# Key latent and narrow columns in one product, and the query latent's norm applied in the softmax's exponential

## Chip, cores and metric

The kernel runs on one core of one Trainium2 chip. The metric is the device time of one execution in microseconds; of several executions the median counts. PE is the matmul engine, PEld its weight load, DVE the vector engine, ACT the scalar (activation) engine, POOL the general engine, SP the engine that issues most DMAs.

## What is computed

Two layers of a trunk with three branches (a state space mixer, latent attention, a gated delta rule), all fed by one input projection of the normed input, 512 tokens by 1024 channels, float32. The change is in latent attention (MLA) and in the projection's columns that feed it:

```python
xn = rmsnorm(x, norm1_g)
proj = xn @ w_in                        # columns: ... c_q 512, c_kv 256, k_rope 64, dt 16, a 8, b 8 ...
q  = (rmsnorm(cq, q_norm_g)   @ w_uq)   # 8 heads of 128 + 64 (rotary)
kv = (rmsnorm(ckv, kv_norm_g) @ w_ukv)  # 8 heads of 128 (key) + 128 (value)
sc = (q_nope @ k_nope.T + rope(q_pe) @ rope(k_rope).T) * (128 + 64) ** -0.5
o  = softmax(causal(sc)) @ v
```

## The kernel before, in words

Every matrix product is made in three parts (L181 to L183, helper `mm3`): a value is split into a high part (ACT, L153 for weights) and a low part (DVE, L154), and high x high, high x low and low x high are summed. Weights come by DMA into `wraw` (two buffers) and are split into `whi` and `wlo` (four buffers each, 512 columns). The normed input stands transposed, features on partitions, as eight tiles `xh`, `xl`, one for each 128 features.

`dense_T` (L217) yields a product with tokens on partitions: the input's 128 tokens are the stationary side, the weights' columns move past. `dense_F` (L187) yields it with features on partitions: 128 weight columns are stationary, all 512 tokens move.

A layer starts with the norm of the input in two halves of 256 tokens (`norm_half`, L286): scaling on DVE (L291), transposes on PE (L296), the split into `xh` (ACT, L260) and `xl` (DVE, L261). To have work while the second half is normed, PE makes with the first half the product of 96 narrow columns (`smalls`, tile `yt`: k_rope, dt, a, b, features on partitions, 256 tokens at a time) and the first four pieces of the query latent's product (512 columns, tokens on partitions). Behind the second half's norm come the rest of the query latent, the four transposes of the narrow columns (L392), and the key latent's product (256 columns, tokens on partitions). Then `latent` (L478) norms both: squares summed on ACT (L485), the scale on DVE and POOL (L264, L265), the scaling on DVE (L489), transposes on PE (L494: 16 for the query, 8 for the key), and a split with the gain (L260, L261).

In layer 0 a table of angles is made in the same time (`rope_tables`, L119, DVE L127 to L144, two sine calls of ACT, L142 and L145), and the step sizes of the other branches are worked out (L404 to L446), from `sv`.

Latent attention follows, four pairs of heads. For each head and each of four token tiles PE makes the scores (L611 to L615) and adds the mask (L616), DVE takes the negated maximum `mx` (L620), ACT the exponential with its sum (L623), DVE the scaling (L624, L625), PE the transposes (L633), and then the product with the values (L649 to L651).

Each engine runs its own list of instructions in order. The lists are made when the kernel is built, by the framework's scheduler: it walks the program and places what it takes to be ready, weight splits with priority. So a stage of the program text can be spread between others, and what stands in a list behind a waiting instruction waits too.

Of the kernel before, what the change touches and what calls it, by code (L numbers as in the profile page):

```python
# [20 lines left out]
P = 128  # L21
# [6 lines left out]
O_SZ, O_XBC, O_DT, O_CQ, O_CKV, O_KR = 0, 1024, 2560, 2576, 3088, 3344  # L28
O_GQ, O_GK, O_GV, O_GZ, O_GB, O_GA, O_GATE = 3408, 3920, 4432, 5456, 6480, 6488, 6496
NBLK = 5  # L30
HALVES = (slice(0, S // 2), slice(S // 2, S))
# [23 lines left out]
def hybrid_kernel(ctx, tc, a, out, depth=2, taps=None):  # L55
# [33 lines left out]
    def y_bank():  # L89
        return mk(ps_sm, [P, 512], F32, "yt", 1)  # L90
# [6 lines left out]

    ct = mk(cst, [P, NBLK * P + 112], F32, "ct")
    sync.dma_start(ct[:, :P], cm[:, :P])
# [116 lines left out]

    def dense_T(gen, n, K, xh, xl, evac, cols=lambda w: w, mid=None, hook=None):  # L217

# [15 lines left out]
        if hook:  # L234
# [6 lines left out]
            return  # L241
        if mid:
            lead = [next(gen) for _ in range(4)]
            for w in lead:
                part(w, (0, 1))
            mid()
            for w in lead:
                part(w, (2, 3))
        for w in gen:
# [61 lines left out]

    def small_raw(ly):

        raw = mk(wp, [P, KD * 96], F32, "wraw", 2)
        sync.dma_start(raw, a["w_small"][ly])
        return raw

    def small_weights(raw, first=True):
        res = []
        for q in range(2):  # L320
            hold = [mk(lp, [P, 384], F32R, "mix", 8) for _ in range(2)]
            hi, lo = split_half(raw[:, q * 384 : (q + 1) * 384], hold, first)
            res.append((4 * q, hi.rearrange("p (k n) -> p k n", k=4), lo.rearrange("p (k n) -> p k n", k=4)))
        return res
# [11 lines left out]
    for t in range(T):  # L336
# [3 lines left out]
        for i in range(2):  # L340
            if t == 2 and i == 1:

                raws0 = small_raw(0), weights_raw(a["w_in"][0], O_CQ, 512, 0, 2)
# [10 lines left out]
    for ly in range(depth):  # L354
# [6 lines left out]


        sw = small_weights(small_raw(ly)) if ly else small_weights(raws0[0], False)
        ps_small = y_bank()

        def smalls(hf):
            for k0, wh, wl in sw:
                for k in range(4):
                    kk = k0 + k
                    mm3(ps_small[:96, hf], wh[:, k, :], wl[:, k, :], xh[kk][:, hf], xl[kk][:, hf], kk == 0, kk == KD - 1)  # L370

        def second_half():
            norm_half(1, [xt[:, t] for t in range(T)], ssq, lambda k: col(g_n1 + k), xpl, xh, xl)
            if ly == 0:
                load_constants()
                load_rows(prow, 0)
            smalls(HALVES[1])

        smalls(HALVES[0])
        cq_tok = [mk(lp, [P, 512], F32, "mix", 8) for t in range(T)]  # L380
        dense_T(weights(w_in, O_CQ, 512, D, raw0=None if ly else raws0[1]), 512, D, xh, xl, lambda t, ps: act.copy(cq_tok[t], ps), mid=second_half)
# [6 lines left out]
        smT = mk(ml, [96, S], F32, "qp")  # L388
        act.copy(smT, ps_small[:96, :])
        ps = sm_bank()  # L390
        for t in range(T):
            pe.transpose(ps[:, t * P : t * P + 96], smT[:, t * P : (t + 1) * P], ident[:96, :96])  # L392
        sv = mk(ml, [P, T, 32], F32, "sv")
        dve.tensor_copy(sv, ps.rearrange("p (t n) -> p t n", t=T)[:, :, 64:96])

# [101 lines left out]

        ck_tok = [mk(lp, [P, 256], F32, "mix", 8) for t in range(T)]
# [14 lines left out]

        kd = mk(lp, [P, S], F32, "mix", 8)
        for i in range(2):
            act.dma_start(kd[64 * i : 64 * i + 64], smT[:64])
        kpe = rope(kd)
# [16 lines left out]
        for hp in range(4):  # L534
# [67 lines left out]
            for j in range(2):  # L602
# [3 lines left out]
                for t in range(T):  # L606
# [655 lines left out]
def lay_out(inputs):  # L1262
# [6 lines left out]
    res["prows"] = np.concatenate([v[n] for n in ROWS], axis=1)  # L1269
    w = np.concatenate([v["w_in"][:, :, c : c + n] for c, n in ((O_KR, 64), (O_DT, 16), (O_GA, 8), (O_GB, 8))], axis=2)  # L1270
    res["w_small"] = np.ascontiguousarray(w.reshape(depth, KD, P, 96).transpose(0, 2, 1, 3)).reshape(depth, P, KD * 96)
    res["cmats"] = shape_constants()
# [17 lines left out]
```

## Time and profile before

| | us |
|---|---|
| median of 3 executions | 2338.18 (2336.49 to 2344.52) |
| span of the profiled execution | 2334.6 |
| PE busy in it | 2294.8 |
| DVE busy | 1582.1 |
| ACT busy | 1159.8 |
| PE waits for latent norms, layer 0 and layer 1 | 2.5 and 1.3 |

The profiled execution is a further one, known by its span from first to last instruction alone; the three timed executions include what lies around the span. The granted matmul clock was 0.996 of full speed in it. How to read: a timeline row has the start, the duration, engine, line, operation, output and inputs, shapes and count, and in brackets the idle time of the engine ahead of it with what ended that. A matmul's duration overlaps the next one's, so a busy PE is not PE at its peak. A waits row has the sum, the count and the longest. SPq is the queue of DMA issues on SP.

### The profile page before, as it was taken

Reading aid. Unit: us, or ns where it says so; the run is one execution under the profiler, and the core shown is the slowest. Engines: PE = TensorE matmul, PEld = TensorE weight load, DVE = VectorE, ACT = ScalarE, POOL = GpSimd, SP = SyncE. Lnnn points to the kernel's source line nnn. Section 1 sums busy time; section 2 is a strip of 40 time slices with the busy share of each in tenths; the row PEclk is TensorE's granted clock in tenths of the full one; section 3 lists DMA queues with packets and bytes.
Section 4 is the critical chain, followed back from the end, with each engine's and each line's share of the span. In section 5 each row is a group of like instructions: output and inputs, shape, how many; then the busy total and the mean of one; then the engine's idle time right before and its main releaser. Section 6 shows DMA issues by size and latency. Waiting matters only on the chain.

```text
span 2334.6 us, 32156 instructions
## 1 busy us (share of the span) xinstructions
PE 2294.8 (98%) x11926; PEld 1891.3 (81%) x11926; DVE 1582.1 (68%) x3100; ACT 1159.8 (50%) x2403; POOL 58.6 (3%) x74
## 2 busy tenths in 40 slices
PE   8999999999999999999999999999999999999998
PEld 7788787878887888888888887888788878888886
DVE  6776656875675458668767765667756645677668
ACT  6656644333443345545656557443334434545545
POOL 0000000000000000000010000000000000000000
PEclk9999999999999999999999999999999999999999
DMA  4323533352222443243132235334422224333231
GB/s 136 87 63 92 169 101 109 109 154 73 86 69 72 140 150 108 73 127 108 44 101 81 82 91 170 101 105 139 118 82 86 68 77 158 126 118 100 91 109 46
DMA packets 208221, 240.38 MB, mean 103 GB/s; under 512 B 33920, under 2 KB 155456, under 8 KB 208064
## 3 DMA queue, kind: packets, MB, share of 16 engines
q1 hardware_dynamic: 204544, 233.07, 32.7%
q10 hardware_dynamic: 3520, 5.25, 0.9%
q8 instruction: 94, 1.54, 0.3%
q14 instruction: 63, 0.52, 0.1%
HBM read 221.41 MB, written 11.63 MB: 100 GB/s over the span
## 4 chain that ended last, share of the span: by engine, by line
PE 86%; DVE 7%; DMA 3%; ACT 2%; POOL 1%; issue 1%; ACTq 0%; SPq 0%; DVEq 0%; POOLq 0%
PE acc L181 22%; PE acc L182 22%; PE acc L183 22%; PE sm L183 2%; PE sm L182 2%; PE sm L181 2%; DVE wlo L154 1%; PE sm L730 1%; DMA eE<-d_c 1%; DVE tok L846 1%; DMA mix<-mix 1%; PE sm L633 1%; DVE gQ L845 1%; PE yt L182 1%; PE sm L1003 1%
## 5 line engine op out<-in xcount | busy, mean ns | idle before, releaser
L154 DVE TENSOR_TENSOR wlo<-wraw,whi 128x512 fp32r<-128x512 f32 x552 | 378.3, 689 | 429.2 <-ACT whi L153 412.4
L153 ACT CAST whi<-wraw 128x512 fp32r<-128x512 f32 x552 | 341.4, 621 | 598.0 <-PE acc L182 371.0
L183 PE MATMUL acc<-xh,wlo 128*128 128x512 f32 (+1 forms) x1184 | 460.9, 390 | 0.0
L181 PE MATMUL acc<-xh,whi 128*128 128x512 f32 (+1 forms) x1184 | 460.7, 390 | 0.0
L182 PE MATMUL acc<-xl,whi 128*128 128x512 f32 (+1 forms) x1184 | 460.0, 389 | 0.0
L183 PEld LDWEIGHTS acc<-xh,wlo 128*128 128x128 f32 x1184 | 223.6, 189 | 41.9
L182 PEld LDWEIGHTS acc<-xl,whi 128*128 128x128 f32 x1184 | 223.5, 189 | 42.0 <-DVE xl L261 0.4
L181 PEld LDWEIGHTS acc<-xh,whi 128*128 128x128 f32 x1184 | 223.2, 189 | 41.7 <-ACT xh L260 0.4
L181 PE MATMUL acc<-yh,whi 128*128 128x512 f32 x384 | 151.9, 399 | 0.0
L182 PE MATMUL acc<-yl,whi 128*128 128x512 f32 x384 | 151.4, 394 | 0.0
L183 PE MATMUL acc<-yh,wlo 128*128 128x512 f32 x384 | 151.3, 394 | 0.0
L183 PE MATMUL acc<-whi,xl 128*128 128x512 f32 (+1 forms) x384 | 144.0, 375 | 0.0
L182 PE MATMUL acc<-wlo,xh 128*128 128x512 f32 (+1 forms) x384 | 143.9, 375 | 0.0
L181 PE MATMUL acc<-whi,xh 128*128 128x512 f32 (+1 forms) x384 | 142.6, 374 | 0.0
L674 DVE SCALAR_TENSOR_TENSOR ckl<-acc,pc,ckl 128x511 f32<-128x511 f32 (+2 forms) x168 | 120.4, 744 | 16.9 <-ACT ckl L670 8.3
L153 ACT CAST whi<-wr 128x512 fp32r<-128x512 f32 x128 | 79.5, 621 | 68.2 <-PE acc L183 32.7
L183 PE MATMUL acc<-whi,yl 128*128 128x512 f32 x256 | 99.7, 389 | 0.0
L181 PE MATMUL acc<-whi,yh 128*128 128x512 f32 x256 | 99.7, 389 | 0.0
L182 PE MATMUL acc<-wlo,yh 128*128 128x512 f32 x256 | 99.6, 389 | 0.0
L154 DVE TENSOR_TENSOR wlo<-wr,whi 128x512 fp32r<-128x512 f32 x128 | 85.8, 686 | 12.5 <-ACT whi L153 11.7
L181 PEld LDWEIGHTS acc<-yh,whi 128*128 128x128 f32 x384 | 71.7, 188 | 16.8 <-ACT yh L260 1.7
L182 PEld LDWEIGHTS acc<-yl,whi 128*128 128x128 f32 x384 | 72.2, 188 | 15.3 <-issue 1.0
(411 smaller groups left out, 4545.3 us busy)
## 6 DMA issues: line engine op xcount, KB each, us to landing
wraw<-in_w_in_dram SPq DMA_DIRECT2D x148, 512.0 KB, 3.6
wraw<-in_w_up_dram SPq DMA_DIRECT2D x64, 512.0 KB, 3.6
wr<-in_w_down_dram SPq DMA_DIRECT2D x32, 1024.0 KB, 5.0
eE<-d_c SPq DMA_DIRECT2D x48, 256.0 KB, 4.0
wraw<-in_w_mla_out_dram SPq DMA_DIRECT2D x16, 512.0 KB, 3.4
eE<-d_e SPq DMA_DIRECT2D x32, 256.0 KB, 3.0
wraw<-in_w_ssd_out_dram SPq DMA_DIRECT2D x16, 512.0 KB, 3.4
wraw<-in_w_gdn_out_dram SPq DMA_DIRECT2D x16, 512.0 KB, 3.3
```

Of the source, the lines that this page charges most:

```text
L153: act.copy(hi, raw)
L154: dve.tensor_tensor(lo, raw, f32(hi), ALU.subtract)
L181: pe.matmul(o, ah, bh, start=start, stop=False, skip_group_check=more)
L182: pe.matmul(o, ah, bl, start=False, stop=False, skip_group_check=more)
L183: pe.matmul(o, al, bh, start=False, stop=stop, skip_group_check=more)
L633: pe.transpose(ps[:, n : n + P], pn[t][:, kb * P : (kb + 1) * P], ident)
L674: dve.scalar_tensor_tensor(acc[:, d:], ps[:, : S - d], taps_[3 - d], acc[:, d:], ALU.mult, ALU.add)
L730: pe.matmul(py[:, h * 64 : (h + 1) * 64], e2[h // 4][:, h % 4, :], xd[:, h * 64 : (h + 1) * 64], start=True, stop=True)
L845: dve.tensor_tensor(pd, bc_last(nb[:, m, m + 1 :], m + 1), bc_mid(xb[:, m, : m + 1], 31 - m), ALU.mult)
L846: dve.tensor_tensor(xb[:, m + 1 :, : m + 1], xb[:, m + 1 :, : m + 1], pd, ALU.add)
L1003: pe.matmul(po[:, h * P : (h + 1) * P], pt_[:, h, :], vn[:, h * P : (h + 1) * P], start=True, stop=True)
```

## The change

- The 64 + 32 narrow columns are joined to the key latent's 256: one product of 352 columns, tokens on partitions, in the place of `smalls` and of the first query pieces. For tokens 0 to 255 it runs while the second half is normed, for the others after it. All eight pieces of its weights stay split: four in `mix` tiles, four in `whi` and `wlo`. The weights are laid out anew in memory (`w_front`) and come in four loads of 360 KB a layer.
- The rotary key's 64 columns are copied twice next to each other out of the product (DVE), and four transposes give the doubled tile `kd`, which two DMAs copied together before. `sv` is copied straight out of the product.
- The query latent is a `dense_F` product in two halves of 256 columns: features on partitions, no transposes. It is split with its gain but without its norm. ACT squares it, DVE adds the four squares up, PE sums them over the partitions against a column of ones, and the result is the scale of each token, `q_rs`. A query's scale is common to a row of scores, so it is applied to the maximum (a new ACT operation) and as the exponential's scale.
- The second half of the query latent's product stands behind the key latent's norm in the text.

```diff
-        sw = small_weights(small_raw(ly)) if ly else small_weights(raws0[0], False)
-        smalls(HALVES[0])
-        cq_tok = [mk(lp, [P, 512], F32, "mix", 8) for t in range(T)]
-        dense_T(weights(w_in, O_CQ, 512, D, ...), 512, D, xh, xl, lambda t, ps: act.copy(cq_tok[t], ps), mid=second_half)
...
+    def front_weights(ly, raws):
+        res = []
+        for q in range(KD // 2):
+            given = q < len(raws)
+            raw = raws[q] if given else front_raw(ly, q)
+            for i in range(2):
+                hold = [mk(lp, [P, NF], F32R, "mix", 8) for _ in range(2)] if q < 2 else None
+                res.append(split_half(raw[:, i * NF : (i + 1) * NF], hold, not given))
...
+        def front(ts):
+            pss = [acc_bank()[:, :NF] for _ in ts]
+            for k, (wh, wl) in enumerate(fw):
+                for t, ps in zip(ts, pss):
+                    tok = slice(t * P, (t + 1) * P)
+                    mm3(ps, xh[k][:, tok], xl[k][:, tok], wh, wl, k == 0, k == KD - 1)
+            for t, ps in zip(ts, pss):
+                act.copy(ck_tok[t], ps[:, :256])
+                dve.tensor_copy(kr_tok[:, t].rearrange("p (i n) -> p i n", i=2), bc_mid(ps[:, 256:320], 2))
+                dve.tensor_copy(sv[:, t], ps[:, 320:])
+        front((0, 1))
+        norm_half(1, ...)
+        front((2, 3))
...
-        dense_T(weights(w_in, O_CKV, 256, D), 256, D, xh, xl, lambda t, ps: act.copy(ck_tok[t], ps))
-        cqh, cql = latent(ml, cq_tok, 512, g_q, "cq")
+        def query_latent(i):
+            for j, ps in enumerate(dense_F(weights(w_in, O_CQ + 256 * i, 256, D), tiles(256), D, xh, xl)):
+                k = 2 * i + j
+                split_gain(cqh[k], cql[k], ps, col(g_q + k))
+                cq_sq.append(mk(ml, [P, S], F32, "pn3", 2))
+                act.activation(cq_sq[-1], ps, AF.Square)
+                if k:
+                    dve.tensor_tensor(cq_sq[0], cq_sq[0], cq_sq[k], ALU.add)
+        query_latent(0)
         ckh, ckl = latent(lp, ck_tok, 256, g_kv, "ck")
...
+        query_latent(1)
+        for t in range(T):
+            pe.matmul(ps[:, t : t + 1], cq_sq[0][:, t * P : (t + 1) * P], ones[:, 0:1], start=True, stop=True)
+        rsq(q_rs, ps[:, :T], 1.0 / 512, EPS)
...
-                    act.activation(pt_[:, :n], o, AF.Exp, bias=mx, accum_out=sm)
+                    act.activation(mx, mx, AF.Copy, scale=q_rs[:, t : t + 1])
+                    act.activation(pt_[:, :n], o, AF.Exp, bias=mx, scale=q_rs[:, t : t + 1], accum_out=sm)
```

Three places show how the lists change. The first is ACT at the start of layer 0, before: `wraw_128` holds the narrow columns, `wraw_130` and `wraw_255` the first query pieces, `hj` are squares of the input's halves.

```order
L153 CAST mix_206<-wraw_128 128x384
L153 CAST mix_210<-wraw_128 128x384
L260 ACTIVATE xh_26_142<-sm_170,pc_121 128x256
L260 ACTIVATE xh_28_144<-sm_179,pc_121 128x256
L260 ACTIVATE xh_30_146<-sm_188,pc_121 128x256
```

And in the change, where `wraw_128`, `130`, `222` and `232` are the four loads of the front, in this order:

```order
L154 CAST whi_224<-wraw_222 128x352
L154 CAST whi_228<-wraw_222 128x352
L254 ACTIVATE xh_30_146<-sm_188,pc_121 128x256
L254 ACTIVATE xh_32_148<-sm_197,pc_121 128x256
L154 CAST mix_218<-wraw_130 128x352
L415 ACTIVATE aexp_1084<-prow_123 128x24
L254 ACTIVATE xh_31_147<-sm_188,pc_121 128x256
L254 ACTIVATE xh_33_149<-sm_197,pc_121 128x256
L154 CAST whi_234<-wraw_232 128x352
L154 CAST whi_238<-wraw_232 128x352
```

The last piece of the second load (`mix_218`) stands behind both pieces of the third, and the fourth load goes into the second one's buffer, which is free when that piece is split.

The second place is PE where the latents are normed in layer 0, before: `mix_239` to `242` are the query latent's token tiles, `acc_744` to `746` the first pair of heads' queries.

```order
L494 MATMUL sm_671<-ct_75,mix_242 128x128
L181 MATMUL acc_744<-cqh_123_649,whi_749 128x512
L181 MATMUL acc_745<-cqh_123_649,whi_749 128x512
L181 MATMUL acc_746<-cqh_123_649,whi_749 128x512
L494 MATMUL sm_678<-ct_75,mix_239 128x128
```

And in the change: `acc_576` is the last tile of the query latent, `yh_68` to `yh_71` the scaled key latent, `yl_72` the rotary key.

```order
L182 MATMUL acc_576<-xh_32_148,whi_629 128x512
L487 MATMUL sm_554<-ct_75,yh_68_242 128x128
L487 MATMUL sm_561<-ct_75,yh_68_242 128x128
L507 MATMUL sm_568<-ct_75,yl_72_246 128x128
L487 MATMUL sm_554<-ct_75,yh_69_243 128x128
...
L507 MATMUL sm_568<-ct_75,yl_72_246 128x128 x3
L183 MATMUL acc_576<-xl_40_156,whi_629 128x512
```

The keys' transposes stand five products ahead of the end of the query latent's 96, and the query's transposes are gone.

The third place is ACT in the first head's softmax, before (`pn` the probabilities of a token tile, `sme` their sum):

```order
L623 ACTIVATE pn_200_930,sme_931<-sm_921,mx_928 128x128
L623 ACTIVATE pn_204_944,sme_945<-sm_935,mx_942 128x256
L623 ACTIVATE pn_208_958,sme_959<-sm_949,mx_956 128x384
L623 ACTIVATE pn_212_972,sme_973<-sm_963,mx_970 128x512
L562 ACTIVATE qh_1227<-acc_1160 128x512
```

And in the change (`qrs` is the query's scale):

```order
L634 ACTIVATE mx_869<-mx_869,qrs_660 128x1
L634 ACTIVATE mx_884<-mx_884,qrs_660 128x1
L635 ACTIVATE pn_196_871,sme_872<-sm_862,mx_869,qrs_660 128x128
L635 ACTIVATE pn_200_886,sme_887<-sm_877,mx_884,qrs_660 128x256
L557 CAST whi_1491<-wraw_1489 128x256
L634 ACTIVATE mx_899<-mx_899,qrs_660 128x1
L558 CAST whi_1491<-wraw_1489 128x128
L635 ACTIVATE pn_204_901,sme_902<-sm_892,mx_899,qrs_660 128x384
```

Each exponential has a second small instruction ahead of it on the same engine and reads what that one wrote.

More of the change, by code (lines that the diff above doesn't have):

```diff
@@ L241, in dense_T @@
             return
[L242 to L248, printed above, removed]
         for w in gen:
@@ L310, in load_rows, with front_raw @@
         sync.dma_start(prow, a["prows"][ly].partition_broadcast(P))
-    def small_raw(ly):
-        raw = mk(wp, [P, KD * 96], F32, "wraw", 2)
-        sync.dma_start(raw, a["w_small"][ly])
+    def front_raw(ly, q):
+        raw = mk(wp, [P, 2 * NF], F32, "wraw", 2)
+        sync.dma_start(raw, a["w_front"][ly][:, 2 * q * NF : 2 * (q + 1) * NF])
         return raw
-    def small_weights(raw, first=True):
+    def front_weights(ly, raws):
         res = []
[L320 to L323, printed above, removed]
+        for q in range(KD // 2):
[4 more added lines that the diff above has]
+                res.append(split_half(raw[:, i * NF : (i + 1) * NF], hold, not given))
         return res
@@ L341, in hybrid_kernel @@
             if t == 2 and i == 1:
-                raws0 = small_raw(0), weights_raw(a["w_in"][0], O_CQ, 512, 0, 2)
+                raws0 = [front_raw(0, q) for q in range(2)]
             hf = slice(i * 512, (i + 1) * 512)
@@ L387, in hybrid_kernel @@
             rope_tables(ml)
[L388 to L394, printed above, removed]
         cum = mk(sp, [P, T, 24], F32, "cum")
@@ L496, in latent @@
             return hs, ls
-        ck_tok = [mk(lp, [P, 256], F32, "mix", 8) for t in range(T)]
-        dense_T(weights(w_in, O_CKV, 256, D), 256, D, xh, xl, lambda t, ps: act.copy(ck_tok[t], ps))
-        cqh, cql = latent(ml, cq_tok, 512, g_q, "cq")
-        ckh, ckl = latent(lp, ck_tok, 256, g_kv, "ck")
+        cqh, cql = hilo_tags(ml, "cq", 4)
+        cq_sq = []
+        def query_latent(i):
[7 more added lines that the diff above has]
+        query_latent(0)
+        ckh, ckl = latent(lp, ck_tok, 256, g_kv, "ck")
+        ps = sm_bank()
+        for t in range(T):
+            pe.transpose(ps[:, t * P : (t + 1) * P], kr_tok[:, t], ident)
+        kd = mk(lp, [P, S], F32, "mix", 8)
+        act.copy(kd, ps)
+        query_latent(1)
+        ps = sm_bank()
+        for t in range(T):
+            pe.matmul(ps[:, t : t + 1], cq_sq[0][:, t * P : (t + 1) * P], ones[:, 0:1], start=True, stop=True)
+        q_rs = mk(sp, [P, T], F32, "qrs")
+        rsq(q_rs, ps[:, :T], 1.0 / 512, EPS)
         def rope(src):
@@ L512, in rope @@
             return ta
-        kd = mk(lp, [P, S], F32, "mix", 8)
-        for i in range(2):
-            act.dma_start(kd[64 * i : 64 * i + 64], smT[:64])
         kpe = rope(kd)
```

31 lines of the change are left out of this document (14 added, 17 removed).

## Prediction

> **What bounds the kernel now.** I read the engines' totals first, then the chain that ended last, then PE's waits around the two places that the change edits.
>
> ```profile
> span 2334.6 us, 32156 instructions
> PE 2294.8 (98%) x11926; PEld 1891.3 (81%) x11926; DVE 1582.1 (68%) x3100; ACT 1159.8 (50%) x2403; POOL 58.6 (3%) x74
> PE 86%; DVE 7%; DMA 3%; ACT 2%; POOL 1%; issue 1%; ACTq 0%; SPq 0%; DVEq 0%; POOLq 0%
> ```
>
> PE carries 86% of the chain and is idle for 39.8 us of 2334.6. So the change is worth what it takes from PE's own work, plus the idle stretches it closes, less those it opens. DVE and ACT matter only where PE stands still for them. PE's waits in the first stage of layer 0 (0 to 215 us), and then of layer 1 (1150 to 1370 us):
>
> ```profile
> PE sm L296 <- DVE xr L291: 1.6, 2, 1.4
> PE sm L494 <- DVE cql L261: 1.2, 1, 1.2
> PE sm L494 <- DVE mix L489: 1.0, 1, 1.0
> PE acc L181 <- ACT cqh L260: 0.3, 1, 0.3
> ...
> PE sm L494 <- DVE mix L489: 1.0, 1, 1.0
> PE acc L181 <- ACT cqh L260: 0.3, 1, 0.3
> ```
>
> The L494 and cqh rows are the latent norms: 2.5 us idle in layer 0 and 1.3 in layer 1, **3.8 us** together. Nothing here is large; the whole stake is some 0.4% of the span.
>
> **PE's work.** Durations of matmuls overlap, so a product's price is its distance to the next one. First and last row of an unbroken stretch of the old query product (66 products), and of the old key product (95):
>
> ```profile
> 29.24 0.39 PE L181 MATMUL acc<-whi,xh 128*128 128x512 f32 x1
> 43.97 0.39 PE L183 MATMUL acc<-whi,xl 128*128 128x512 f32 x1
> 44.68 0.28 PE L182 MATMUL acc<-wlo,xh 128*128 128x256 f32 x1
> 55.96 0.28 PE L183 MATMUL acc<-whi,xl 128*128 128x256 f32 x1
> ```
>
> 65 distances of 512 columns take 14.73 us, 0.227 each; 94 of 256 take 11.28, 0.120 each. A column is thus (0.227 - 0.120)/256 = 0.00042 us, and a product of 352 columns, which the trace does not show, 0.160 by interpolation. Per layer 48 narrow and 96 key products of 256 columns (17.3 us) become 96 of 352 (15.4 us): -1.9. The query product keeps its 96 products of 512 columns; only which side is stationary changes. Next, the transposes:
>
> ```profile
> 56.08 1.47 PE L494 MATMUL sm<-ct,mix 128*128 128x128 f32 x12
> 57.84 0.96 PE L181 MATMUL acc<-cqh,whi 128*128 128x512 f32 x3 [0.29 <-ACT cqh L260]
> 60.02 0.66 PE L494 MATMUL sm<-ct,mix 128*128 128x128 f32 x4 [1.22 <-DVE cql L261]
> 60.43 0.48 PE L182 MATMUL acc<-cql,whi 128*128 128x512 f32 x1
> 60.74 0.40 PE L183 MATMUL acc<-cqh,wlo 128*128 128x512 f32 x1
> 63.95 0.63 PE L494 MATMUL sm<-ct,mix 128*128 128x128 f32 x4 [0.95 <-DVE mix L489]
> L935 PE MATMUL sm<-ct,ft 128*128 128x1 f32 x64 | 7.5, 242 | 0.0
> ```
>
> Four transposes hold PE for 0.41 us (60.02 to 60.43), and the product behind them takes 0.31 in place of 0.227. Sixteen of the query latent go: -1.6 a layer. The four transposes of the narrow columns stay as four of another shape: 0. Four sums of squares against a column of ones come, shown in kind at L935 at most 0.24 each: 0 to 1.0 a layer, and I take 0.5 with the switch. In the softmax the scheduler now cuts the transposes into 35 and 34 groups for 29 and 29, 11 more switches at 0.09: +1.0. Sum: 2 x (-1.9 - 1.6 + 0.5) + 1.0 = **-5.0 us**.
>
> The Trainium skill ("TensorE: Matmul & The Clock Gate", Part 4: PE-mode transpose) gives about 275 ns for a transpose in one kernel's context. By that estimate the 32 transposes would be worth 8.8 us and not 3.2, and the result 5.6 us lower. The trace gives the same duration, but twelve end within 1.47 us, so they overlap and the distance decides.
>
> **The start of layer 0** gets worse. The front now needs all eight pieces of weights before the second half's transposes, four loads where two are in flight, and the fourth load waits for the second one's last split.
>
> ```profile
> 10.22 0.93 ACT L153 CAST mix<-wraw 128x384 fp32r<-128x384 f32 x2 [0.21 <-DMA wraw<-in_w_small_dram]
> 10.77 1.03 DVE L154 TENSOR_TENSOR mix<-wraw,mix 128x384 fp32r<-128x384 f32 x2 [0.17 <-ACT mix L153]
> 11.82 0.38 SPq L160 DMA_DIRECT2D wraw<-in_w_in_dram  x1
> DMA to landing us min/median/max: 3.1/3.8/7.0
> 23.02 1.36 PE L296 MATMUL sm<-ct,xr 128*128 128x128 f32 x11
> ```
>
> The third load leaves as at 11.8 and lands 3.1 to 3.8 later, near 15.2. In ACT's order its two casts (0.45 each) and two activations stand ahead of the cast of the fourth piece, which ends at 17.5, its subtraction on DVE at 18.1. The fourth load leaves then, lands near 21.6, and with cast and subtraction its low half is there at 22.6. Eleven products at 0.160 follow: PE reaches the transposes at 24.4 where it was at 23.02, with 7.7 us of products done where it had 8.3. New idle time: 1.4 + 0.6 = **+2.0** (0 if the load lands in the minimum and the casts wait less; 3 with a late landing). Layer 1 has its weights early; there the fourth group of transposes waits instead:
>
> ```profile
> 1174.54 0.28 PE L181 MATMUL yt<-xh,mix 128*96 128x256 f32 x1
> 1176.56 1.25 DVE L261 SCALAR_TENSOR_TENSOR xl<-sm,pc,xh 128x256 fp32r<-128x256 f32 x3
> ```
>
> From 1174.54 the new order has ten products (1.6 us) ahead of it, and the low half it waits for ends near 1177.0: **+0.9** (0 to 1.5).
>
> **The key latent's norm** is now covered by the second half of the query product, but in layer 0 its scaling stands on DVE behind the table of angles.
>
> ```profile
> 33.18 0.69 DVE L154 TENSOR_TENSOR wlo<-wraw,whi 128x512 fp32r<-128x512 f32 x1
> 33.78 0.69 DVE L139 SCALAR_TENSOR_TENSOR qh<-qh,qh 128x512 f32<-128x512 f32 x1
> 39.29 0.43 DVE L136 TENSOR_SCALAR qh<-qh 128x512 f32<-128x512 f32 x1
> 50.09 0.17 DVE L264 TENSOR_SCALAR lrs<-lss 128x4 f32<-128x4 f32 x1 [3.62 <-ACT pn L485]
> 51.46 1.67 DVE L489 TENSOR_SCALAR mix<-mix,lrs 128x512 f32<-128x512 f32 x4 [1.20 <-POOL lrs L265]
> 56.26 1.72 DVE L416 SCALAR_TENSOR_TENSOR spe<-spe,spq 128x96 f32<-128x96 f32 x6
> ```
>
> With transposes at 24.4 the front ends at 33.8 (16 transposes and 48 products at 0.160), the query product's first half at 44.7. On DVE stand, from the first query piece's low half (from 31.8, once its buffer is free and its cast done) to the key's scale: 21 operations of two inputs and 512 columns at 0.60, eight of one input at 0.40, sixteen of the step sizes at 0.26, and copies, a reciprocal and half pieces for 3.3, together 23.3 us. So the scale comes at 55.1, and 1.4 later (50.09 to 51.46) the scaling, its first tile near 56.8. PE reaches the keys' transposes after 43 products of the second half, near 54.5: **+2.2** (0 if DVE runs 10% faster than these distances, 4 if ACT's two sine calls come late). In layer 1 without the angles: **+0.5** (0 to 1). The 3.8 us of old gaps go, since the query latent needs no norm ahead of its use.
>
> **The softmax.** Each of the 64 score tiles gets a small ACT operation between maximum and exponential, and the exponential a second operand per partition.
>
> ```profile
> 18.03 0.26 ACT L422 ACTIVATE aexp<-prow 128x24 f32<-128x24 f32 x1
> 46.98 0.72 ACT L142 ACTIVATE sinT<-qh,inv_c 128x512 f32<-128x512 f32 x1
> 47.60 0.61 ACT L145 ACTIVATE cosT<-qh 128x512 f32<-128x512 f32 x1
> 87.49 0.23 PE L616 MATMUL sm<-am_b,id_b 128*128 128x128 bf16 x1
> 89.49 0.49 DVE L625 TENSOR_SCALAR pn<-pn,sme 128x512 f32<-128x512 f32 x1
> 90.04 0.76 PE L633 MATMUL sm<-ct,pn 128*128 128x128 f32 x5
> ```
>
> A scale per partition costs 0.11 (sinT against cosT). So the small operation takes 0.33, its signal 0.06 (89.98 to 90.04), the exponential 0.11 more: 0.50 a tile, 32 us of added latency and some 25 us of ACT, which is 50% busy. PE arrives at the transposes just when the tile is ready, 2.55 us behind the mask product. Nothing is spare there; but the scheduler has placed more products between: at the distances above the last tile of a head had 2.50 to 3.84 us of them and now has 2.95 to 3.46, where 2.50 + 0.50 = 3.0 are needed. I take **+1.0** (0 to 32).
>
> The Trainium skill ("ScalarE: Activation LUTs", What ACT_TABLE_LOAD costs) says that each pointer operand of an activation adds about 93 ns. This speaks against the change, and the trace agrees with 0.11 us.
>
> **Sum.** -5.0 - 3.8 + 2.0 + 0.9 + 2.2 + 0.5 + 1.0 = -2.2 us. Against the profiled execution that is a span of 2332.4. The median of the three runs shown, 2338.2, lies 3.6 above that span; with the same difference the time is **2336.0**.
>
> **Rivals.** *The new waits do not come*, as the loads land early and DVE keeps up: -8.8, 2329.4. For it: PE's rows show no wait for weights today. Against it: the fourth load's wait is in the order. *The exponential becomes PE's wait*, ending on the other side: it decides once the products put between fall short of 3.0 us a tile. At the last tile of each of 16 heads alone 0.5 each gives +8 in place of +1, 2343; at all 64 tiles +32, 2367. For it: the arrival is exact now. Against it: the 2.95 to 3.46 us counted. *DVE is late by 4 in layer 0 and the loads by 3*: +2.8, 2338.8. That the change does nothing of what it says is excluded: PE's order has 60 instructions fewer in each layer.
>
> **Chances.** Forecast 0.62 (2332 to 2340), no new waits 0.14, exponential 0.14, DVE and loads late 0.10. About 0.3%, 7 us, is what a measurement of this kernel can tell from no change. Faster by more (under 2331.2): the second case and little else, 0.15. Slower by more: most of the third, 0.12. The rest, 0.73, is within. The range runs from the second case less 1.4 for the median's scatter (the runs shown lie 1.7 below to 6.3 above theirs) to 2345, which leaves out most of the all-tiles case.
>
> **What would show it.** Transposes of the second half in layer 0 at 24.4; a PE wait of some 2 us at the keys' transposes in layer 0 and none over 1 us in layer 1; no L494-like gap after them; PE waits for the softmax's transposes under 1 us in all. I am wrong if PE waits for probabilities by several us, or if the 352-column product does not run at 0.160.

## The result, and the profile after

Over 20 executions of each, the changed kernel takes 2335.64 us in the median (2329.51 to 2339.86) and the kernel before 2337.80 (2332.73 to 2345.65): a ratio of **0.9988 (0.9979 to 0.9996)**; the medians lie 2.2 us apart. That is within 0.3%, and the forecast of 2336.0 is 0.4 us off. (A ratio with an interval is formed over all executions, here and below; it is not the quotient of the two medians.) The page of the changed kernel (span; busy time, share and count of each engine; shares of the chain that ended last):

```profile
span 2335.7 us, 32023 instructions
PE 2294.3 (98%) x11814; PEld 1889.9 (81%) x11814; DVE 1586.4 (68%) x3116; ACT 1177.1 (50%) x2455; POOL 59.5 (3%) x74
PE 88%; DVE 6%; DMA 2%; ACT 2%; POOL 1%; issue 1%; ACTq 0%; SPq 0%; DVEq 0%; POOLq 0%
```

This one execution has a longer span than the one of before (2334.6), at a granted clock of 0.994 against 0.996; the medians say more than the two spans. PE is the bound as it was, with 112 matmuls fewer (11926 to 11814). Its waits from 0 to 215 us, where the start (L290), the rotary queries (L625), the keys' transposes (L487) and the products of the transposed, split probabilities with the values (L661, L662) stand:

```profile
PE sm L290 <- DVE xr L285: 3.0, 2, 2.7
PE sm L625 <- ACT qps L591: 1.3, 1, 1.3
PE sm L487 <- DVE yh L482: 0.9, 1, 0.9
PE yt L661 <- ACT mix L250: 0.8, 1, 0.8
PE yt L662 <- DVE mix L251: 0.4, 1, 0.4
```

From 1150 to 1370 us, layer 1:

```profile
PE sm L625 <- ACT qps L591: 3.1, 2, 1.9
PE sm L487 <- DVE yh L482: 1.3, 1, 1.3
...
PE sm L290 <- DVE xl L255: 0.5, 1, 0.5
```

The L661 and L662 rows are there again, with the same 0.8 and 0.4. The old gaps at the latent norms are gone, and those at the keys' transposes are 0.9 and 1.3 us. One wait has grown that no step had a price for: L625 waits for `qps`, the rotary part of a pair's queries, for 4.4 us in three places. The same wait in before and in the change, whole execution:

```profile
PE sm L614 <- ACT qps L580: 1.9, 3, 0.9
```

```profile
PE sm L625 <- ACT qps L591: 4.4, 3, 1.9
```

### The profile page after: what moved, and what is told of

Its sections match the earlier page's. It is cut to its first block, busy times and chain, and to the rows that moved or that the text cites. A ratio compares the mean times of both kernels' runs of the same rounds, so it can differ in the third digit from the quotient of the medians.

```text
span 2335.7 us, 32023 instructions
## 1 busy us (share of the span) xinstructions
PE 2294.3 (98%) x11814; PEld 1889.9 (81%) x11814; DVE 1586.4 (68%) x3116; ACT 1177.1 (50%) x2455; POOL 59.5 (3%) x74
## 4 chain that ended last, share of the span: by engine, by line
PE 88%; DVE 6%; DMA 2%; ACT 2%; POOL 1%; issue 1%; ACTq 0%; SPq 0%; DVEq 0%; POOLq 0%
PE acc L182 23%; PE acc L184 22%; PE acc L183 22%; PE sm L184 2%; PE sm L182 2%; PE sm L183 2%; DVE wlo L155 1%; PE sm L742 1%; DMA eE<-d_c 1%; PE sm L645 1%; DVE tok L858 1%; DVE gQ L857 1%; PE sm L1015 1%; POOL gms L259 1%; PE yt L661 1%
## 5 line engine op out<-in xcount | busy, mean ns | idle before, releaser
L155 DVE TENSOR_TENSOR wlo<-wraw,whi 128x512 fp32r<-128x512 f32 (+1 forms) x552 | 376.6, 686 | 420.8 <-ACT whi L154 401.5
L154 ACT CAST whi<-wraw 128x512 fp32r<-128x512 f32 (+1 forms) x552 | 339.9, 618 | 593.1 <-PE acc L183 383.6
L184 PE MATMUL acc<-xh,wlo 128*128 128x512 f32 (+1 forms) x1248 | 486.8, 390 | 0.0
L182 PE MATMUL acc<-xh,whi 128*128 128x512 f32 (+1 forms) x1248 | 486.1, 390 | 0.0
L183 PE MATMUL acc<-xl,whi 128*128 128x512 f32 (+1 forms) x1248 | 485.1, 389 | 0.0
L184 PEld LDWEIGHTS acc<-xh,wlo 128*128 128x128 f32 x1248 | 235.8, 189 | 44.9 <-issue 0.3
L183 PEld LDWEIGHTS acc<-xl,whi 128*128 128x128 f32 x1248 | 235.8, 189 | 44.4 <-DVE xl L255 0.4
L184 PE MATMUL acc<-whi,xl 128*128 128x512 f32 (+1 forms) x288 | 111.2, 386 | 0.0
L183 PE MATMUL acc<-wlo,xh 128*128 128x512 f32 (+1 forms) x288 | 111.1, 386 | 0.0
L182 PE MATMUL acc<-whi,xh 128*128 128x512 f32 (+1 forms) x288 | 110.3, 385 | 0.0
```

Source lines behind the costliest of these rows:

```text
L154: act.copy(hi, raw)
L155: dve.tensor_tensor(lo, raw, f32(hi), ALU.subtract)
L182: pe.matmul(o, ah, bh, start=start, stop=False, skip_group_check=more)
L183: pe.matmul(o, ah, bl, start=False, stop=False, skip_group_check=more)
L184: pe.matmul(o, al, bh, start=False, stop=stop, skip_group_check=more)
```

## The experiments

Three series, each on one chip with its own executions of the kernel before. Each execution lists the mean matmul clock granted to it, 0.991 to 0.999, and the times follow it: 1.58, 1.66 and 1.84 us per 0.001 in the three series. As differences of 2 us are at stake, each kernel is also given **at equal clock**: its distance from the kernel before on lines of that slope, fitted to all executions of a series (they scatter by 1.3 to 1.6 us around them), with a 95% interval. What a kernel itself does to its clock is left out of these numbers: query_only and front_only had a mean clock of 0.993 where the kernel before had 0.997, and in the medians they are 19.0 and 14.6 us slower, not 13.6 and 8.1. Kernels of different series are compared through the kernel before alone.

| kernel | median (before) | ratio | at equal clock, us |
|---|---|---|---|
| change_again | 2335.86 (2338.29) | 0.9999 (0.9986 to 1.0011) | -2.3 ± 0.9 |
| query_only | 2355.51 (2336.48) | 1.0089 (1.0076 to 1.0102) | +13.6 ± 1.8 |
| front_only | 2351.09 (2336.48) | 1.0062 (1.0050 to 1.0074) | +8.1 ± 1.9 |
| noscale | 2334.41 (2336.48) | 0.9995 (0.9985 to 1.0006) | -3.1 ± 1.2 |
| warm | 2335.95 (2336.48) | 1.0003 (0.9994 to 1.0012) | -1.6 ± 1.1 |
| early | 2341.54 (2335.49) | 1.0021 (1.0008 to 1.0034) | +0.9 ± 1.0 |
| mxdve | 2340.43 (2335.49) | 1.0022 (1.0012 to 1.0032) | +3.2 ± 1.0 |
| rotary | 2331.02 (2335.49) | 0.9981 (0.9969 to 0.9994) | -5.4 ± 0.9 |
| best | 2331.38 (2335.49) | 0.9978 (0.9968 to 0.9988) | -3.0 ± 0.9 |
| rotary_early | 2330.89 (2338.29) | 0.9976 (0.9963 to 0.9988) | -6.2 ± 0.9 |
| rotary_warm | 2331.75 (2338.29) | 0.9979 (0.9965 to 0.9993) | -4.3 ± 0.9 |
| poolq | 2331.66 (2338.29) | 0.9977 (0.9966 to 0.9988) | -7.3 ± 0.9 |

### The two halves of the change, each alone

`query_only` is the kernel before with the query latent's part of the change; the narrow columns and the key keep their own products.

```diff
-        cq_tok = [...]; dense_T(weights(w_in, O_CQ, 512, D, ...), ..., mid=second_half)
+        cq_ps = dense_F(weights(w_in, O_CQ, 256, D, ...), tiles(256), D, xh, xl, mid=second_half)
...
-        cqh, cql = latent(ml, cq_tok, 512, g_q, "cq")
         ckh, ckl = latent(lp, ck_tok, 256, g_kv, "ck")
+        query_latent(1, dense_F(weights(w_in, O_CQ + 256, 256, D), tiles(256), D, xh, xl))
```

> The query part alone: narrow columns and key latent as before, the query latent with features on partitions, its norm in the exponential. My theory, that the parts' prices add as in the two traces: 16 transposes fewer and the ones-matmuls at the 0.81 us measured, -0.8 a layer; the half of the query product that covers the second norm in pieces of 256 columns, +0.6 a layer; the old norm gaps -3.8 in all; softmax and rotary query later, +3 in all. Sum -1 us against before (-3 to +1). Rival: the whole gain comes from the joined product, and this is slower than before by 2 us or more.

Measured +13.6. PE's longest wait in it:

```profile
PE sm L631 <- ACT qps L597: 10.6, 5, 3.3
```

The theory's -1 is missed by far. 8.7 us of the 13.6 are the rotary queries' wait (10.6 against 1.9); the other 4.9 are not taken apart.

`front_only` is the change with the query latent as it was: tokens on partitions, its norm ahead of its use.

```diff
-        query_latent(0)
+        cq_tok = [...]; dense_T(weights(w_in, O_CQ, 512, D), 512, D, xh, xl, lambda t, ps: act.copy(cq_tok[t], ps))
         ckh, ckl = latent(lp, ck_tok, 256, g_kv, "ck")
...
-        query_latent(1)
...
+        cqh, cql = latent(ml, cq_tok, 512, g_q, "cq")
...
-                    act.activation(mx, mx, AF.Copy, scale=q_rs[:, t : t + 1])
-                    act.activation(pt_[:, :n], o, AF.Exp, bias=mx, scale=q_rs[:, t : t + 1], accum_out=sm)
+                    act.activation(pt_[:, :n], o, AF.Exp, bias=mx, accum_out=sm)
```

> The joined product of 352 columns alone; the query latent with tokens on partitions, with 16 transposes and its norm ahead of its use, as before, nothing in the exponential. My theory: the joined product takes away the work that stood between the query latent's product and its transposes, so PE waits there for squares, scale and scaling, 4 to 6 us a layer where before 1.3 to 2.5 were lost. With -3.8 of product work and +2.8 at the starts the sum is +4 us against before (0 to +8). Rival: the parts simply add, and with a query part of -1 this gives -2.

Measured +8.1. Its longest wait:

```profile
PE sm L487 <- DVE mix L482: 10.0, 2, 5.0
```

The query's norm now follows its product at once, and PE stands still for 5.0 us in each layer, as the theory had it, where before's rows of this kind had 1.0 each. The excess of 8.1 is as large as the loss; what else the kernel wins and loses cancels. So neither half saves anything alone, and the two together do (-2.3). The parts can't be added up: the joined product takes away the work that covered the query's norm, and only the other half of the change makes that norm unnecessary ahead of the query's use.

### The exponential's small operation

`noscale` leaves out this operation and the exponential's second operand, so the query's norm is not applied.

```diff
-                    act.activation(mx, mx, AF.Copy, scale=q_rs[:, t : t + 1])
-                    act.activation(pt_[:, :n], o, AF.Exp, bias=mx, scale=q_rs[:, t : t + 1], accum_out=sm)
+                    act.activation(pt_[:, :n], o, AF.Exp, bias=mx, accum_out=sm)
```

> The change without its softmax part: the small operation and the exponential's second operand are left out, so the query latent's norm is not applied (it leaves out that scale). My theory: PE's waits at the softmax's transposes and their products fall from 2.7 us to about 0.7 in the two layers, -2 us against the change (0 to -3), and ACT is less busy by some 25 us. Rival, that the exponential stands on PE's path at the last tile of each head or at all tiles: -8 to -32 us.

0.8 ± 1.5 us less than the change (-3.1 against -2.3, two series): that fits the forecast's +1.0 and also nothing at all, and rules out 8 or 32. Two rows of it, where lines from 634 on are one lower:

```profile
PE sm L625 <- ACT qps L591: 5.6, 4, 2.7
...
PE yt L661 <- DVE mix L251: 0.5, 2, 0.2
```

The waits for the split probabilities are 0.5, against 2.4 in the L661 and L662 rows of both layers above; but the rotary queries' wait is 1.2 longer (5.6 against 4.4). 1.9 less 1.2 is about what was measured. `mxdve` moves the small operation to DVE instead:

```diff
-                    act.activation(mx, mx, AF.Copy, scale=q_rs[:, t : t + 1])
+                    dve.tensor_scalar(mx, mx, q_rs[:, t : t + 1], None, ALU.mult)
```

> The change with the maximum scaled on DVE, behind its reduction, in place of ACT. My theory: a DVE operation of this size takes about 0.16 us and the ACT one 0.29, and a handover between engines goes, so each tile's chain is shorter by 0.1 to 0.2 us; PE's waits at the softmax's products (1.6 and 0.9 us) fall to about half, -1 us against the change (0 to -2). Rival, that the exponential's second operand and its length set that wait: no difference in the waits.

+3.2, which is 5.5 above the change. Its `qps` wait is 8.2 against 4.4, in four places; the rest is not explained, nor why the lists turn out so.

### The start

The profile of the change showed PE still for 2.7 us ahead of the first transposes and then a low clock. `warm` fills the stillness with 12 more products of the warm-up.

```diff
-    for i in range(16):
+    for i in range(28):
         pe.matmul(warm[:, :P], ident, ident, start=True, stop=True)
```

> The change with 28 in place of 16 warm-up products, so that PE is busy until its first transposes. In the profile of the change PE stood still for 2.7 us ahead of them, and had half its clock from 12.4 to 19.2 us. Theory that the stillness brings the low clock: the clock is full from the first transposes on, the products of the first half cost 0.160 each and not 0.295, and PE then waits for the fourth load's pieces; the second half's transposes stand at 22.5 to 23.5 us in place of 24.36, -1 to -2 us. Rival, that the low clock comes by chance: it is seen again, or was not there in most runs, and the time is the same within 0.5 us.

The low clock did not appear in its profile, but PE is at the warm-up until the transposes, and these begin later than the change's 10.60:

```profile
6.72 5.25 PE L331 MATMUL yt<-ct 128*128 128x128 f32 x38
11.81 0.93 PE L290 MATMUL sm<-ct,xr 128*128 128x128 f32 x7
```

-1.6 ± 1.1 against -2.3 ± 0.9: no gain is shown.

The same kernel as the change, run once more (`change_again`), separates the low clock from the change's own work.

> The change itself once more, on the chip of the three others and beside the kernel before, so that the others have it for comparison. Expected: 2 to 3 us under the kernel before, as in its first runs (ratio 0.9988), and waits for the rotary query of 3 to 6 us.

-2.3 at equal clock, and in the medians -2.4 (the mean clock of its executions was 0.9955, that of before 0.9962). The ratio of this series, 0.9999, does not tell the change from nothing; only the equal clock does. Its start is read below.

### The key's norm

`early` puts the key latent's squares, scale and scaling ahead of the table of angles.

```diff
         ml = mp.enter_context(tc.tile_pool(name="ml", bufs=1, reuse_waits="tile"))
+        ck_ss = mk(sp, [P, T], F32, "lss")
+        for t in range(T):
+            act.activation(jk, ck_tok[t], AF.Square, accum_out=ck_ss[:, t : t + 1])
+        rsq(ck_rs, ck_ss, 1.0 / 256, EPS)
+        for t in range(T):
+            dve.tensor_scalar(ck_tok[t], ck_tok[t], ck_rs[:, t : t + 1], None, ALU.mult)
         if ly == 0:
```

> The change with the key latent's squares, scale and scaling ahead of the query latent's product and of the table of angles. My theory: PE's waits of 0.9 and 1.3 us at the key latent's transposes go, and the time falls by 2.2 us against the change. Rival, drawn from the run with the query part alone, where PE waited 10.6 us for the rotary query: what PE gains ahead of the first scores it waits for there, so the waits for the rotary query grow by as much, and the time stays within 0.5 us.

The L487 wait is gone, as it should be, and the kernel is slower than the change, +0.9 against -2.3:

```profile
PE sm L625 <- ACT qps L591: 7.7, 4, 2.7
```

PE came to the rotary queries sooner and waited there. The wait moved, as the rival had it: 2.2 us given for 3.3. That is 1.1 of the 3.2 it lost; the rest is not explained.

### The rotary queries

Why they are late shows on ACT at the third pair of heads in the change. `qp` is the rotary tile out of PE's product, the ACTq rows are the first and the last of the four copies of its parts that ACT issues:

```profile
119.82 0.61 ACT L580 ACTIVATE qp<-acc 128x512 f32<-128x512 f32 x1
131.91 0.55 ACTq L521 DMA_DIRECT2D mix<-qp  x1
...
135.75 0.59 ACT L250 CAST yh<-yt 128x512 fp32r<-128x512 f32 x1 [2.66 <-PE yt L663]
135.76 0.51 ACTq L521 DMA_DIRECT2D mix<-qp  x1
```

`qp` is there at 120.43 and the first copy leaves 11.5 us later. In that time ACT works through casts and the exponentials of the next head, which stand ahead of the copy in its list; it stands still for only 1.8 us of it. The last copy leaves with a cast (L250, of a finished head's output) for which ACT stood still 2.66 us: an issue waits in ACT's list like any instruction. Behind that, at 145.62, PE stood still for the 1.3 us of the row from 0 to 215 us above.

Two edits follow. `rotary` makes the rotary tile of a pair first and rotates it ahead of the heads' own tiles.

```diff
-            *pq, pp = dense_F(q_weights(), tiles(384), 512, cqh, cql)
+            pp, *pq = dense_F(q_weights(), tiles(384)[2:] + tiles(384)[:2], 512, cqh, cql)
...
-            qs = head_tiles(pq, "q", scale)
             qp = mk(ml, [P, S], F32, "qp")
...
             qr = rope(qp)
+            qs = head_tiles(pq, "q", scale)
```

> The change with the rotary columns of a pair's query first in each product, and their copy and rotation ahead of the casts of the two heads' queries. My theory: PE's waits for the rotary query (4.4 us in the profile of the change, 1.9 before) come from a chain that starts too late; the rotary product ends 1.4 us earlier and its copy stands ahead of one or both 0.6 us casts, so the waits fall to 1 to 2 us, -2.5 to -3.5 us against the change. Rival, that the copies land late because two weight loads share the transfers with them: the chain starts earlier but ends at the same time, waits of 3.5 us or more, 0 to -1 us.

-5.4, or 3.1 ± 1.3 better than the change. Its `qps` wait is 3.2 in four places, not the 1 to 2 of the theory: that is 1.2 of the 3.1. The L661 and L662 waits fall too, from 2.5 in the whole execution to 0.5, and a wait of PE for `vl` (L251) grows from 0.6 to 2.6; the sum is not explained.

`rotary_early` and `rotary_warm` add the edits of `early` and of `warm` (22 products), `best` both and `mxdve`'s.

> The rotary columns first, as in that run, and the key latent's norm early, as in that run. Alone the first made the change faster by 3.5 us and the second slower by 2.7 (at an equal clock). Theory that the early norm only brought PE sooner to the wait for the rotary query: with that wait shortened the 2.2 us at the key latent's transposes are won, -1 to -2 us against the rotary run alone. Rival, that the early norm costs by its own place in the lists of ACT and DVE: +2 to +3 us against the rotary run.

> The rotary columns first, and 22 warm-up products. In the rotary run PE stood still for 1.8 us ahead of its first transposes and had half its clock for 3.4 us. Theory that stillness brings the low clock: no low clock at the start, -1 us against the rotary run (0 to -2). Rival: a low clock at the start all the same, or no gain.

> All three together, and 22 warm-up products. If the prices add: -2.2 for the key latent's norm, -2.5 for the rotary query, -1 for the maximum, -1 for the clock at the start: about 6 us under the change, 8 to 9 under the kernel before (0.3 to 0.4%). If the waits only move to the next place: within 2 us of the change.

-6.2, -4.3 and -3.0 beside rotary's -5.4, from two series. `early`, which lost by itself, no longer loses: rotary_early is 0.8 ± 1.3 better than rotary, not told from nothing, and its `qps` wait is down to one:

```profile
PE sm L625 <- ACT qps L591: 0.7, 1, 0.7
```

The warm-up brings nothing here either. `best` is 2.4 worse than rotary at equal clock (0.4 in the medians, as its clock was higher) though its `qps` wait is only 1.1; `mxdve`, which lost alone too, is in it.

`poolq` leaves the order and lets POOL, 3% busy, issue the copies.

```diff
-                act.dma_start(sw_[32 * i : 32 * i + 32], src[32 * (i ^ 1) : 32 * (i ^ 1) + 32])
+                pool.dma_start(sw_[32 * i : 32 * i + 32], src[32 * (i ^ 1) : 32 * (i ^ 1) + 32])
...
-                act.dma_start(qd[64 * i : 64 * i + 64], qr[64 * (1 - i) : 64 * (1 - i) + 64])
+                pool.dma_start(qd[64 * i : 64 * i + 64], qr[64 * (1 - i) : 64 * (1 - i) + 64])
```

> The change with the copies of the rotary query and key issued by POOL in place of ACT. In the change's third pair of heads the fourth of four copies leaves 2.6 us behind the third, since it is queued on ACT behind a cast that waits for PE. My theory: that queue makes the rotary query late; POOL has nothing to wait for, so PE's waits for it fall from 4.4 us to under 2, -2 to -3 us against the change. Rival: an issue from POOL takes longer and the copies land later; waits of 5 us or more and no gain.

-7.3, 5.0 ± 1.1 better than the same kernel with the copies on ACT in the same series: the fastest at equal clock, and faster than both kernels. The third pair again, ACT and POOL:

```profile
116.17 0.60 ACT L580 ACTIVATE qp<-acc 128x512 f32<-128x512 f32 x1
121.89 1.97 POOL L521 DMA_DIRECT2D mix<-qp  x4 [12.85 <-PE yt L663]
```

All four copies leave within 7.1 us of `qp`, where ACT needed 15.8 to the last (120.43 to 136.27). POOL has something to wait for as well, other than the theory said: 5.1 of its 7.1 us it waits for PE's L663, which reads split probabilities out of `mix`, the buffers that the copies write. PE's waits:

```profile
PE sm L625 <- ACT qps L591: 2.5, 2, 1.8
```

2.1 us less than in change_again (4.6), and the L661 and L662 waits (2.4 above) are not there, with 0.6 at the transposes of the probabilities in their place: some 4 of the 5.0. How much is the list that the copies stood in, and how much the time that their issues took from ACT's softmax, was not separated.

The Trainium skill ("DMA: Bandwidth & Descriptors", Issuing engines are not separate DMA queues) says that issuing from another engine only saves the sequencer's time for the issue, which is usually small beside the transfer. Here it was worth 5.0 us in all. What was seen to go with it is a delay of another kind: the first copy left 11.5 us behind its input on ACT, in a list with a head's softmax ahead of it, and 5.1 us behind it on POOL.

## Why the prediction came out right, step by step

The total was right; its parts were not all. Prices are read from the page of the change and from change_again, whose clock was full at the start.

| step | forecast | measured |
|---|---|---|
| 352-column product, pitch | 0.160 | 0.160 |
| narrow columns in one product, a layer | -1.9 | -1.7 |
| 16 transposes, a layer | -1.6 | -1.7, -1.6 |
| column of ones, a layer | +0.5 | +0.8 |
| switches in the softmax | +1.0 | about 0 |
| old norm gaps | -3.8 | gone |
| start, layer 0 | +2.0 | -0.3 (change_again) |
| start, layer 1 | +0.9 | +0.5 |
| key's norm, both layers | +2.7 | +2.2 |
| softmax's waits | +1.0 | about +2.4 |
| rotary queries' wait | none | +2.5 to +2.7 |

**PE's work** held. The pitch, from 23 distances in the change, (24.20 - 20.52)/23, makes 15.4 us of 96 products; at their own distances in before (0.118 and 0.120) the 48 narrow and 96 key products are 17.2:

```profile
20.52 0.32 PE L182 MATMUL acc<-whi,xh 128*128 128x352 f32 x1
24.20 0.32 PE L184 MATMUL acc<-whi,xl 128*128 128x352 f32 x1
24.36 1.36 PE L290 MATMUL sm<-ct,xr 128*128 128x128 f32 x11
62.71 0.95 PE L513 MATMUL sm<-ct,pn 128*128 128x1 f32 x8
63.52 0.49 PE L184 MATMUL acc<-cqh,wlo 128*128 128x512 f32 x1
```

The last two rows are the sums against ones: PE is held for 0.81 where 0.5 was taken, as the four of the program are eight matmuls in the trace.

**The start of layer 0 is the step that failed.** The forecast had the second half's transposes at 24.4, because the fourth load of weights would wait for the second one's last split, and the row above has them at 24.36. That looks like proof and is none. In the change's first 25 us:

```profile
10.60 0.55 PE L290 MATMUL sm<-ct,xr 128*128 128x128 f32 x3 [2.70 <-DVE xr L285]
12.99 0.49 PE L183 MATMUL acc<-mix,xh 128*128 128x352 f32 x1
13.29 0.49 PE L182 MATMUL acc<-mix,xh 128*128 128x352 f32 x1
```

and in its windows (length, busy time and count of PE, PEld, DVE, ACT, POOL, then PE's clock, DMA share, GB/s):

```profile
12.00:20.00 8.00, 7.57 (x32) 6.87 (x31) 6.96 (x19) 6.36 (x19) 1.10 (x2) 0.57 0.54 142
```

The products stand 0.30 apart instead of 0.160, with a clock of 0.57: 0.43 of 8 us, or 3.4 us of clock. In change_again the clock there is full:

```profile
12.00:20.00 8.00, 6.66 (x41) 5.87 (x40) 6.77 (x19) 6.18 (x19) 1.10 (x2) 1.00 0.62 164
```

and the rows of PE, of the third load's subtraction, of the fourth load on SP, of the second load's last cast, of the fourth load's cast and subtraction, and the wait of the SP queue ahead of the fourth load are

```profile
9.72 0.55 PE L290 MATMUL sm<-ct,xr 128*128 128x128 f32 x3 [0.38 <-DVE xr L285]
15.23 0.96 DVE L155 TENSOR_TENSOR wlo<-wraw,whi 128x352 fp32r<-128x352 f32 x2 [0.17 <-ACT whi L154]
16.22 0.33 SPq L309 DMA_DIRECT2D wraw<-in_w_front_dram  x1
16.22 0.48 ACT L154 CAST mix<-wraw 128x352 fp32r<-128x352 f32 x1
19.18 0.88 ACT L154 CAST whi<-wraw 128x352 fp32r<-128x352 f32 x2 [1.63 <-DMA wraw<-in_w_front_dram]
19.70 0.96 DVE L155 TENSOR_TENSOR wlo<-wraw,whi 128x352 fp32r<-128x352 f32 x2 [0.76 <-ACT whi L154]
22.16 0.38 PE L290 MATMUL sm<-ct,xr 128*128 128x128 f32 x2
SPq L309 <- DVE wlo L155: 1.5, 1, 1.5
```

The load leaves at 16.22, not 18.1, right behind the third load's last subtraction (16.19), while the second load's last cast only begins. So it takes the third load's buffer, not the second's, which the order of the lists does not show: the forecast's reading of it was wrong. The change's own profile has the same row of the SP queue, with the load at 17.05 behind a subtraction that ends at 17.02, and the second load's last cast at 17.90. In change_again the low half of the load is there at 20.66, not 22.6, PE has no wait for weights in its list of waits, and the transposes come at 22.16, 0.9 before those of the kernel before (23.02). With 7.7 us of products done by then where it was 8.3, the start costs -0.9 + 0.6 = -0.3, not +2.0.

The price for the load was for a wait that does not exist, and that the number agreed in the change's profile is luck. Of the 2.2 us between 22.16 and 24.36, 0.9 is a later start (10.60 against 9.72 for the first transposes) and 1.3 the low clock, which nobody had forecast; part of the 3.4 us is covered by a wait for `xh` that falls from 1.33 to 0.43.

**The key's norm** had its size and not its place: 0.9 and 1.3 where 2.2 and 0.5 were forecast. In the change's layer 0 the scale comes at 53.83 and the scaling at 55.22, earlier than the 55.1 and 56.8 forecast, since DVE kept up. In layer 1 it is later, because the squares (L478) stand on ACT behind the query latent's work and wait for DVE's sum of its squares (`pn`, L501):

```profile
1206.44 0.42 ACT L478 ACTIVATE pn<-yh 128x256 f32<-128x256 f32 x1 [0.26 <-DVE pn L501]
1208.61 0.17 DVE L258 TENSOR_SCALAR lrs<-lss 128x4 f32<-128x4 f32 x1 [1.67 <-ACT pn L478]
1210.39 0.96 PE L487 MATMUL sm<-ct,yh 128*128 128x128 f32 x6 [1.33 <-DVE yh L482]
```

**The rotary wait** was not in the sum, though before's profile had its row (1.9). Its growth is mostly layer 1's. There the second of two copies of the first pair leaves at 1234.6 and lands 5.1 us later, where the median of these copies is 2.4:

```profile
1234.10 1.15 ACTq L585 DMA_DIRECT2D mix<-mix  x2
1239.71 0.61 ACT L591 CAST qps<-mix 64x512 fp32r<-64x512 f32 x1 [2.51 <-DMA mix<-mix]
```

A load of 512 KB of weights leaves beside it, at 1234.54. That the two share the transfers, as the rival to `rotary` had it, is likely here and was not tested.

**So the total came out by compensation.** The first row of the next stage, PE's first L763 (L775) behind DVE's `tok`, in before:

```profile
274.03 0.33 PE L763 MATMUL yt<-ct,tok 128*128 128x128 f32 x1 [0.64 <-DVE tok L758]
1433.05 0.33 PE L763 MATMUL yt<-ct,tok 128*128 128x128 f32 x1 [0.58 <-DVE tok L758]
```

and in change_again:

```profile
271.00 0.33 PE L775 MATMUL yt<-ct,tok 128*128 128x128 f32 x1 [0.70 <-DVE tok L770]
1432.38 0.33 PE L775 MATMUL yt<-ct,tok 128*128 128x128 f32 x1 [0.58 <-DVE tok L770]
```

The stage of layer 0 is 3.0 us shorter, and 2.4 of it is given back by the second row (0.67 left). Where, the first rows of layer 1 show, in before and in change_again:

```profile
1170.84 0.55 PE L296 MATMUL sm<-ct,f 128*128 128x128 f32 x3 [0.49 <-DVE f L291]
```

```profile
1168.34 0.55 PE L290 MATMUL sm<-ct,f 128*128 128x128 f32 x3 [0.49 <-DVE f L285]
```

Up to there lies code that the change leaves alone, and change_again is 0.5 us longer in it. 1.6 us of that is clock, and a wait at L742 (L730 in before) that is shorter by 0.9 stands against it. The larger of two stretches with a low clock, in before and in change_again:

```profile
510.00:530.00 20.00, 18.24 (x359) 13.83 (x358) 6.52 (x11) 10.92 (x19) 0.00 (x0) 0.74 0.54 112
```

```profile
505.00:525.00 20.00, 18.14 (x352) 14.03 (x351) 6.65 (x12) 9.01 (x15) 0.00 (x0) 0.66 0.60 136
```

Before lost 5.2 us here and change_again 6.8; the other stretch, in layer 1, has 0.91 over 20 us in both. From the start of layer 1 to the second row before takes 262.2 us and change_again 264.0. So layer 0 gave -3.0 where the terms of the forecast come to -0.3, and layer 1 gave +1.8 where they come to -1.9, with the softmax's shared evenly. The measured terms of the table come to -3.0 and +1.6. The total of the forecast, -2.2, was met because an error of 2.7 us in layer 0 and one of 3.7 in layer 1 stand against each other: what was priced for layer 0's load and did not come pays for part of the rotary and softmax waits, above all layer 1's. That is luck. The two layers give -1.2 in this profile and the code between them another -1.1 without its clock; behind the second row change_again takes 1.2 us longer, which is not explained. The table's -1.4 in all is at the edge of the -2.3 ± 0.9. Not in it is a wait of 0.7 us in each layer of before (PE for `qp`, L569) that the change no longer has.

**The rivals.** That the new waits don't come (2329.4) was half right: the load's did not, others did. The exponential as PE's wait (2343, 2367) is refuted by noscale. DVE and loads late (2338.8) is refuted by change_again's rows.

## What to carry to other kernels

A total that agrees proves no step: read each step at its own place and layer, on a second execution too, before you believe its mechanism. A cover given to one wait sends the bound engine sooner to its next one, here a rotary copy issued from a busy in-order list; an edit that loses alone (`early`) can stop losing once that next wait is mended. Here small transfers on the way to the bound engine were best issued from an engine whose list holds little else.

## What the runs showed of the hardware

- **A low clock after a short stillness, sometimes.** Of the six profiles in which PE stood still for 1.8 us or more ahead of the first transposes, two have a low clock behind it (2.70 us still: 0.66 in the mean over 10 to 20 us; 1.83: 0.83), four have none (1.84, 1.90, 2.12, 2.16), and none of the eight with less (0 to 1.45). The Trainium skill ("TensorE: Matmul & The Clock Gate", Part 1) has the clock halve after an idle window of about 3.4 us that runs freely, so that runs differ. The chance in it agrees; 1.83 us is shorter than such a window, and what sets it off, or whether the transposes behind the stillness count as work, is not settled here. The stretches near 510 us begin the same way: PE stands still for 1.76 us in before and for 1.86 in change_again, waiting for a transfer (L879, L891), and the clock is then 0.50 to 0.54 for 10 us.
- **The mean clock** differs from execution to execution, from 0.991 to 0.999, and 0.001 is 1.6 to 1.8 us of these 2335. It is as large as the effect of the change.
- **An issue of a copy takes 0.5 to 0.6 us** on ACT (0.51 and 0.55 above) and 0.5 on POOL (four in 1.97). Near 132 us casts of ACT ran beside the issues; at 1231.05 ACT had stood still for 1.83 us behind them.
- **Left open:** what in `mxdve` makes the lists worse, and whether the change itself lowers the mean clock (0.9955 against 0.9962 in one series, 0.9962 over its first 20 executions), and whether the long stillnesses of query_only and front_only lowered theirs (0.993).
